# Another order of pools and tiles in SBUF for a transformer kernel on one core

## The chip, the cores and the metric

The kernel runs on one core of one Trainium2 chip. The metric is device time in microseconds of one execution; the time before is the median of three runs, 2584.69 us (2582.28 to 2592.01). TensorE is called PE here, its weight load PEld, VectorE DVE, ScalarE ACT, GpSimd POOL, and the queue that issues the DMAs SP.

## The reference

Two transformer stacks are computed for 256 tokens of width 1024, one after the other. The first has two layers with a context of 256 more tokens (differential and neighbourhood attention, then grouped-query attention; a SwiGLU feed-forward after each). The second has four layers; each is a mixer, a cross-attention to a memory, and a convolved feed-forward, with a layer norm after each:

```python
def swiglu(h, w1, w3, w2):
    return (jax.nn.silu(h @ w1) * (h @ w3)) @ w2

qkv = x @ w_qkv                                   # grouped-query mixer of the second stack
q, k, v = jnp.split(qkv, [A_HEADS * A_HEAD_DIM, (A_HEADS + A_KV_HEADS) * A_HEAD_DIM], axis=-1)
```

Everything is float32. Nearly all of the work is `activation @ weight` with a weight matrix that is read once from DRAM.

## The kernel before, in words

Each large product is made of three matrix products of a cheaper number format (float32r): weight and activation are split into a high and a low part, and `mm3` (L130 to 134) adds high times high (L132), one cross product (L133) and the other (L134). `weights` (L117 to 128) loads 1 MB of a weight matrix into a `raw` buffer by one DMA from SP, and splits it in four quarters: ACT writes `whi` (L126), DVE writes `wlo` (L127). The activations stand transposed, features on partitions, as a pair of tiles high and low (`Th`, `Tl`, in the first phase `xTh`, `xTl`), made by `pair` (L160).

There are two forms of product. In one the weights are the stationary operand (128 columns of `whi` or `wlo`) and the activations move past them, 256 or 512 columns: all "up" products of the feed-forwards, the queries of the cross-attention, the projections of the recurrent layer. In the trace this is `bank<-Th,whi`: the moving operand comes first, the stationary one second. In the other the activations are stationary and 512 columns of weights move (`bank<-whi,Th`, `bank<-whi,hh`): attention projections, output projections, and the "down" products, whose activations `hh`, `hl` are small tiles of the hidden units. `fp32_groups` (L100) does the first two chunks of a stage in plain float32 from `raw` and `xv`.

The program goes through four phases. A (to about 350 us): first mixer. B (350 to 752): feed-forward of 512 tokens, products with 512 moving columns. C (752 to 932): grouped attention with context, and the memory's keys and values. D (932 to the end): the feed-forward of layer two and the whole second stack, 256 tokens. PE's order is the program's order; SP is one queue in order.

SBUF is given out as two stacks that grow towards each other: pools open on the left, from byte 16512 of each partition, or with `side="right"` downwards from byte 229344. A pool that is opened later takes the bytes that a closed pool gave back, and its tiles then wait for the last use of the tiles that overlap them. Left, in order, stand the constants `cp` (19584 bytes), `sm` (1568), `wk` (10240), then per phase `wraw` (`raw`, three buffers of 8 KB), `whl` (`whi` and `wlo`, two buffers of 8 KB each in A and C, three in B and D), then the phase's other tiles. In A and B the activations `xTh`, `xTl`, `Th`, `Tl` are on the right (190.6 to 222.6 KB); in D they are on the left (two pairs, 134.8 to 166.8 KB), with the weights at 70.8 to 118.8 KB. These places are the pools' sizes added up in their order. One thing follows: every left tile behind `sm` begins 32 bytes past a multiple of 128, every right tile 96 bytes past one.

Of the kernel before, what the change touches and what calls it, by code (L numbers as in the profile page):

```python
# [12 lines left out]
F32R = mybir.dt.float32r  # L13
# [45 lines left out]
class Net:  # L59
# [12 lines left out]
    def fill(self, n=1):  # L72
        """Emits n more steps of the work that waits for gaps."""
        while n and self.work:
            if next(self.work[0], None) is None:
                self.work.popleft()
            else:
                n -= 1
# [5 lines left out]
    def flush(self):  # L84
        """Emits the transposes held back until the matrix products that run before them are emitted."""
        while self.held:
            self.held.popleft()()

    def update(self):
        """Emits what is left of the last normalisation: the rows for the next one."""  # L90
        while self.updates:
            self.updates.popleft()()

    def bank(self, tag):
        """A bank of PSUM; several tags: each in turn."""
        i = self.turn[tag] = self.turn.get(tag, -1) + 1
        tag = tag[i % len(tag)]
        return self.psum.tile([P, 512], F32, tag=tag, name="bank" + tag, bufs=1 if tag in "to" else 2)

    def fp32_groups(self, banks, raws, xv, n):  # L100
        """banks[i][:, n-th group of 256, tokens] = raw[:, :, n-th 128 columns]^T @ x, first rows first."""
        for t in range(2):
            ts = slice(t * P, (t + 1) * P)
            for i, (ps, r) in enumerate(zip(banks, raws)):
                for f in range(n):
                    if t or n * i + f == FLUSH:
                        self.flush()
                    for k in range(KD):
                        self.nc.tensor.matmul(ps[:, f * S + t * P : f * S + (t + 1) * P],
                                              r[:, k * n * P + f * P : k * n * P + (f + 1) * P], xv[:, k, ts],  # L110
                                              start=k == 0, stop=k == KD - 1)
# [48 lines left out]
    def pair(self, tag, width):  # L160
        hi = self.tp.tile([P, KD, width], F32R, tag=tag + "h", name=tag + "h")
        lo = self.tp.tile([P, KD, width], F32R, tag=tag + "l", name=tag + "l")
        return hi, lo
# [15 lines left out]
    def fm_rows(self, src, t, n, dst, xv=None, scale=None, bias=None, banks="to", later=None):  # L179
        """Rows src [128, 512] (features 512 n on), transposed, into dst (hi, lo) [:, 4 n.., col]; with xv  # L180
        times scale plus bias by feature, and into xv, too."""
        nc = self.nc
        ps = self.bank(banks[n])
        for i in range(4):
            self.transpose(ps[:, i * P : (i + 1) * P], src[:, i * P : (i + 1) * P])
        hi, lo = (d[:, 4 * n : 4 * n + 4, t * P : (t + 1) * P] for d in dst)
        if xv is None:
            self.split(ps.rearrange("p (k q) -> p k q", k=4), hi, lo)
            return
        for i in range(4):  # L190
            k = 4 * n + i
            p, o = ps[:, i * P : (i + 1) * P], xv[:, i, :]
            if n:
                nc.vector.tensor_scalar(o, p, scale[:, k : k + 1], bias[:, k : k + 1], op0=ALU.mult, op1=ALU.add)
            else:
                nc.scalar.activation(o, p, AF.Identity, scale=scale[:, k : k + 1], bias=bias[:, k : k + 1])
        if later is None:
            self.split(xv, hi, lo)
        else:
            later.append((xv, hi, lo))  # L200

    def modulated(self, src, dst, t, a, b, xv=None, banks="to"):
        """dst (hi, lo) [:, :, t-th tile] = transpose(rms(src)) * a + b; src: a row tile."""
# [11 lines left out]
    def normed_rows(self, src, xv):  # L215
        """xv [128, 8, tokens] = transpose(rms(src)), not yet scaled; src: row tiles."""
# [9 lines left out]
    def scaled(self, xv, dst, cols, a, b):  # L226
        """dst (hi, lo) [:, :, cols] = xv * a + b by feature; xv is overwritten."""
        nc = self.nc
        for k in range(KD):
            x = xv[:, k, cols]  # L230
            (nc.vector if k % 2 else nc.gpsimd).tensor_scalar(x, x, a[:, k : k + 1], b[:, k : k + 1], op0=ALU.mult, op1=ALU.add)
            nc.scalar.activation(dst[0][:, k, cols], x, AF.Copy)
            nc.vector.tensor_tensor(dst[1][:, k, cols], x, dst[0][:, k, cols].bitcast(F32), op=ALU.subtract)

    def conv(self, dst, ps, o, step, n):
        """Two halves of a bank, each with its causal filter of n + 1 taps and bias at o, o + step of fm."""
# [9 lines left out]
    def rope(self, dst, src, width, kind, t):  # L246
        """dst = src * cos + rotated(src) * sin, rows by heads of 64; kind: 0 axial, 1 halves."""
# [88 lines left out]
    def memory(self, pool):  # L336
        """Yields after each chunk of weights."""
# [29 lines left out]
    def ada(self, l, p):  # L367
        """Yields after each chunk of weights; mods[l, p]: by feature, gate rows in DRAM."""
# [42 lines left out]
    def pair_attn(self, q, k, nk, v, out, bias=None, sink=None):  # L411
        """q, k, v: functions of the head's half (v of the key tile, too), q and k as one or as [hi, lo]; out:
        [128, 128] of a bank."""
# [42 lines left out]
    def mixer_ab(self, xT, first, ap, inner, oA, later, after):  # L456
        """ap: pool in inner, which is closed when xT and the first heads are done; later: makes what follows."""
# [140 lines left out]
    def out_ab(self, half):  # L598
        """Weights of half of the rows."""
# [3 lines left out]
    def gated_out(self, oT, ws, res, gate):  # L603
        """res += gate * (o @ w), a row tile; yields after each half of the columns."""
# [11 lines left out]
    def swiglu4(self, xT, res, gates, after):  # L616
        """Hidden units of the first layer's FFN for 512 tokens; res[tt] += gate * out."""
# [48 lines left out]
    def gqa(self, xT, w_qkv, kind, sink, cT=None):  # L666
        """Projections, attention; yields the heads' outputs (hi, lo) by feature tiles."""
# [5 lines left out]
        oT = self.pair("T", S)  # L673
# [107 lines left out]
    def quad_attn(self, qT, kT, v, J, t, g, ops, sink):  # L781
        """Heads (j, i) = 2 x 2 of windowed attention: query tile t, keys of tile t and the one before."""
# [39 lines left out]
    def project(self, parts, w_o, nch, done):  # L822
        """parts yields ((hi, lo), chunks ready); done(t, the two banks of o @ w_o) for each row tile."""
# [38 lines left out]
    def layer_norm(self, i, X, new, last=False, rows=False):  # L862
        """done() for project and ffn: X = norm(ALPHA X + banks), transposed into new() = ((hi, lo), xv);
        rows: (hi, lo) come first, else xv."""
# [124 lines left out]
    def cross(self, xT, xv, w_q):  # L989
        nc = self.nc  # L990
        oT = self.pair("T", S)
# [71 lines left out]
    def rglru(self, xT, xv):  # L1063
        nc, A, fm = self.nc, self.A, self.fm
        uf = self.at.tile([P, KD, S], F32, tag="uf", name="uf", bufs=1)
        uT = self.pair("T", S)
# [52 lines left out]
        oT = self.pair("T", S)  # L1119
# [19 lines left out]
    def mla(self, xT):  # L1139
# [69 lines left out]
        oT = self.pair("T", S)  # L1209
# [69 lines left out]
def tile_kernel(ctx: ExitStack, tc: tile.TileContext, A: dict, out: bass.AP):  # L1279
# [5 lines left out]
    net.cp = sub(ctx, "cp")  # L1285
    net.sm = sub(ctx, "sm", 4)
    net.dr = ctx.enter_context(tc.tile_pool(name="dr", bufs=1, space=DRAM))
    net.wk = sub(ctx, "wk", 2)
# [9 lines left out]
    def scope(name, raw, hl):  # L1298
        st = ExitStack()
        net.wraw = sub(st, name + "r", raw)  # L1300
        net.whl = sub(st, name + "s", hl)
# [3 lines left out]
    with ExitStack() as right:  # L1305
        net.pa = sub(right, "pa", side="right")
        with scope("wA", 3, 2) as st:
            inner, late = ExitStack(), ExitStack()
            xT = [sub(inner, "xT" + n, side="right").tile([P, KD, 2 * S], F32R, name="xT" + n) for n in "hl"]
# [33 lines left out]
            def later():  # L1343
                net.drain()
                net.tp = sub(right, "tA", side="right")
# [12 lines left out]
            def after(tt, oB):  # L1358
# [3 lines left out]
                if tt == NAORD[1]:  # L1362
                    net.drain()
                    ws.append(net.out_ab(1))
                    new.extend(net.pair("T", 2 * S))
# [13 lines left out]
        with scope("wB", 3, 3) as st:  # L1379
# [7 lines left out]
            def after(tt):  # L1387
                if tt == 0:
                    net.drain()
                    new.extend(net.pair("T", 2 * S))  # L1390
# [24 lines left out]
    net.tp = sub(ctx, "tC", 2)  # L1415
    xvp = sub(ctx, "xv")
    newv = lambda: xvp.tile([P, KD, S], F32, tag="xv", name="xv")
    xT, xv = net.pair("T", S), newv()
# [5 lines left out]
    def new():  # L1424
        cur[:] = net.pair("T", S), newv()
# [41 lines left out]
def _cols(w, kt, n):  # L1467
    """[K, N] -> [N / n, K / (128 kt), 128, kt * n]"""
# [5 lines left out]
def _rows(w, kt=2):  # L1474
    """[K, N] -> [K / (128 kt), 128, kt * N]"""
# [4 lines left out]
def _fm(v):  # L1480
    """[n] -> [128, n / 128]"""
# [37 lines left out]
def _qkv(w):  # L1519
    """Query columns in the order of _HEADS, keys and values first."""  # L1520
# [8 lines left out]
def _updown(a, b):  # L1529
    """Two [1024, 2816] side by side in tiles of 128 columns: [22, 128, 2048]"""  # L1530
# [4 lines left out]
def _na_bias(rpb):  # L1535
    """[8, 15, 31] -> [4, 2, 128, 2, 256]: by query and key of the 4 x 64 grid"""
# [91 lines left out]
```

## Time and profile before

| | |
|---|---|
| median of three runs | 2584.69 us |
| profiled execution, span | 2586.1 us |
| PE busy | 2487.0 us, 96% |
| DVE, ACT, POOL busy | 1716.6, 1213.8, 224.4 us |
| DMA | 410 MB read, 161 GB/s over the span |

The span of the profiled execution is 0.05% above the median of the runs, so sums made against it hold for the median. A matmul's duration in the profile is longer than the step from its start to the next one's start, since matmuls are pipelined: 256 columns show 0.28 us and follow each other at 0.12 us. Steps are therefore read from the start times of a timeline.

### The profile page before, as it was taken

To read this page: it belongs to the slowest core of one execution; us is meant where nothing else is said; L and a number is where in the kernel's file an instruction comes from. 1 tells how busy PE (TensorE), PEld (TensorE's weight loads), DVE (VectorE), ACT (ScalarE), POOL (GpSimd) and SP (SyncE) were. 2 spreads that over 40 slices of the span, in tenths; PEclk is the share of its full clock that TensorE was granted. 3 is DMA by queue.
4 is the path that set the end of the run, shared out by engine and by line. 5 is a ranking of instruction groups with operands and counts; after the bars stand their busy time and mean duration, and the time that the engine had idled before them with its cause. 6 is when DMAs were issued, how large, how long until landed. Compare 5 with 4: busy or idle time off the path is not lost.

```text
span 2586.1 us, 39903 instructions
## 1 busy us (share of the span) xinstructions
PE 2487.0 (96%) x15706; PEld 2113.6 (82%) x15706; DVE 1716.6 (66%) x3535; ACT 1213.8 (47%) x2628; POOL 224.4 (9%) x222
## 2 busy tenths in 40 slices
PE   6999999999999999999999988999999999999998
PEld 4867677777778789976899987899878899668998
DVE  5463763334368755478677788677876777886777
ACT  3242442222245554456355565465554455554554
POOL 1000011111100000001100121100102100111000
PEclk8999999999999999999999989999999999999999
DMA  7415234443324355553355445345445455433553
GB/s 319 163 56 213 86 135 171 153 165 142 139 95 150 132 215 183 187 180 119 134 196 183 162 177 196 137 177 193 141 146 186 147 195 180 163 115 133 201 189 114
DMA packets 65612, 418.26 MB, mean 162 GB/s; under 512 B 7424, under 2 KB 9728, under 8 KB 18960
## 3 DMA queue, kind: packets, MB, share of 16 engines
q1 hardware_dynamic: 65424, 415.71, 44.6%
q8 instruction: 123, 2.02, 0.3%
q14 instruction: 65, 0.53, 0.1%
HBM read 410.41 MB, written 5.28 MB: 161 GB/s over the span
## 4 chain that ended last, share of the span: by engine, by line
PE 84%; DVE 9%; ACT 2%; issue 2%; POOL 1%; DMA 1%; POOLq 0%; SPq 0%; DVEq 0%; ACTq 0%
PE banka L132 9%; PE banka L133 9%; PE banka L134 9%; PE banks L134 6%; PE banks L132 6%; PE banks L133 6%; PE bankb L134 5%; PE bankb L132 5%; PE bankb L133 4%; DVE wlo L127 4%; PE bankt L158 3%; PE banko L132 2%; PE banko L134 2%; PE banko L133 2%; PE bankt L133 2%; PE bankt L132 2%
## 5 line engine op out<-in xcount | busy, mean ns | idle before, releaser
L127 DVE TENSOR_TENSOR wlo<-raw,whi 128x512 fp32r<-128x512 f32 (+1 forms) x1184 | 831.7, 729 | 315.5 <-ACT whi L126 312.0
L126 ACT ACTIVATE whi<-raw 128x512 fp32r<-128x512 f32 (+1 forms) x1184 | 662.3, 620 | 669.6 <-issue 179.2
L134 PE MATMUL banks<-Th,wlo 128*128 128x256 f32 x880 | 250.5, 285 | 2.6 <-DVE wlo L127 2.6
L132 PE MATMUL banks<-Th,whi 128*128 128x256 f32 x880 | 250.2, 284 | 0.0
L133 PE MATMUL banks<-Tl,whi 128*128 128x256 f32 x880 | 250.1, 284 | 0.0
L134 PEld LDWEIGHTS banks<-Th,wlo 128*128 128x128 f32 x880 | 169.8, 193 | 3.4 <-DVE wlo L127 3.4
L132 PEld LDWEIGHTS banks<-Th,whi 128*128 128x128 f32 x880 | 170.0, 193 | 0.9
L133 PEld LDWEIGHTS banks<-Tl,whi 128*128 128x128 f32 x880 | 170.0, 193 | 0.8
L133 PE MATMUL banka<-wlo,Th 128*128 128x512 f32 (+1 forms) x304 | 121.6, 403 | 3.6 <-DVE wlo L127 3.6
L132 PE MATMUL banka<-whi,Th 128*128 128x512 f32 (+1 forms) x304 | 123.1, 408 | 1.8 <-ACT Th L150 1.6
L134 PE MATMUL banka<-whi,Tl 128*128 128x512 f32 (+1 forms) x304 | 119.8, 401 | 4.7 <-DVE Tl L151 4.7
L646 DVE TENSOR_TENSOR sg<-sg,bankb 128x512 f32<-128x512 f32 x22 | 15.1, 688 | 164.6 <-PE bankb L134 164.6
L132 PE MATMUL bankt<-Th,whi 128*128 128x256 f32 x424 | 120.3, 284 | 0.0
L132 PE MATMUL banko<-Th,whi 128*128 128x256 f32 x424 | 120.0, 283 | 0.0
L134 PE MATMUL bankt<-Th,wlo 128*128 128x256 f32 x424 | 120.0, 283 | 0.0
L134 PE MATMUL banko<-Th,wlo 128*128 128x256 f32 x424 | 120.0, 283 | 0.0
L133 PE MATMUL banko<-Tl,whi 128*128 128x256 f32 x424 | 120.0, 283 | 0.0
L133 PE MATMUL bankt<-Tl,whi 128*128 128x256 f32 x424 | 120.0, 283 | 0.0
L168 POOL TENSOR_SCALAR rs<-mv 128x1 f32<-128x1 f32 x24 | 7.5, 312 | 1240.3 <-DVE mv L882 1240.2
L132 PE MATMUL bankb<-Th,whi 128*128 128x256 f32 (+1 forms) x344 | 114.9, 335 | 0.0
L134 PE MATMUL bankb<-Th,wlo 128*128 128x256 f32 (+1 forms) x344 | 114.7, 334 | 0.0
L133 PE MATMUL bankb<-Tl,whi 128*128 128x256 f32 (+1 forms) x344 | 114.3, 332 | 0.0
(483 smaller groups left out, 6476.3 us busy)
## 6 DMA issues: line engine op xcount, KB each, us to landing
raw<-in_f_w_up_dram SPq DMA_DIRECT2D x88, 1024.0 KB, 4.8
raw<-in_ffn_w_dram SPq DMA_DIRECT2D x66, 1024.0 KB, 4.9
adaw<-in_ada_w_dram SPq DMA_DIRECT2D x48, 1024.0 KB, 4.9
raw<-in_f_w_down_dram SPq DMA_DIRECT2D x44, 1024.0 KB, 4.9
raw<-in_x_w_q_dram SPq DMA_DIRECT2D x16, 1024.0 KB, 5.0
raw<-in_x_w_o_dram SPq DMA_DIRECT2D x16, 1024.0 KB, 5.0
raw<-in_w_in_ab_dram SPq DMA_DIRECT2D x12, 1024.0 KB, 6.2
raw<-in_a_w_qkv_dram SPq DMA_DIRECT2D x12, 1024.0 KB, 4.9
```

The costliest lines, as they stand in the source:

```text
L126: nc.scalar.activation(hi[:, a:b], r[:, a:b], AF.Copy)
L127: nc.vector.tensor_tensor(lo[:, a:b], r[:, a:b], hi[:, a:b].bitcast(F32), op=ALU.subtract)
L132: mm(out, l[0], r[0], start=start, stop=False)
L133: mm(out, l[0], r[1], start=False, stop=False)
L134: mm(out, l[1], r[0], start=False, stop=stop)
L158: self.nc.tensor.transpose(out, src, self.ident[:k, :k])
L168: nc.gpsimd.tensor_scalar(rs, ssum, scale, eps, op0=ALU.mult, op1=ALU.add)
L646: nc.vector.tensor_tensor(sg, sg, ps[1], op=ALU.mult)
```

## The change

One tile `T` of 32 KB, on the right and opened first, takes all activation pairs; `pair` hands out its halves in turn (or the whole, for 512 tokens). Within it, high and low parts of a pair stand one behind the other. In phase C alone the attention's output still has a pool of its own (`tB`, one tile of 16 KB). The pools `cp`, `sm` and `wk` move to the right, below `T`. In each phase's `scope` the split weights `whl` are opened before `wraw`, so they begin at the left end.

```diff
-    def pair(self, tag, width):
-        hi = self.tp.tile([P, KD, width], F32R, tag=tag + "h", name=tag + "h")
-        lo = self.tp.tile([P, KD, width], F32R, tag=tag + "l", name=tag + "l")
-        return hi, lo
+    def pair(self, width):
+        if self.tp is not None:
+            x = self.tp.tile([P, 2 * KD * width], F32R, tag="T", name="T")
+        else:
+            i = self.turn["T"] = self.turn.get("T", -1) + 1
+            n = 2 * KD * width
+            o = i * n % (4 * KD * S)
+            x = self.acts[:, o : o + n]
+        x = x.rearrange("p (a k w) -> p a k w", a=2, k=KD)
+        return x[:, 0], x[:, 1]
...
-    net.cp = sub(ctx, "cp")
-    net.sm = sub(ctx, "sm", 4)
+    net.acts = sub(ctx, "act", side="right").tile([P, 4 * KD * S], F32R, name="T")
+    net.tp = None
+    net.cp = sub(ctx, "cp", side="right")
+    net.sm = sub(ctx, "sm", 4, side="right")
...
-    net.wk = sub(ctx, "wk", 2)
+    net.wk = sub(ctx, "wk", 2, side="right")
...
         st = ExitStack()
+        net.whl = sub(st, name + "s", hl)
         net.wraw = sub(st, name + "r", raw)
-        net.whl = sub(st, name + "s", hl)
         return st
...
-            xT = [sub(inner, "xT" + n, side="right").tile([P, KD, 2 * S], F32R, name="xT" + n) for n in "hl"]
+            xT = net.pair(2 * S)
...
-                net.tp = sub(right, "tA", side="right")
...
-    net.tp = sub(ctx, "tC", 2)
+    net.tp = None
```

The calls `pair("T", n)` become `pair(n)`; the rest of the diff takes comments out. No instruction, transfer or order of the program is added or removed.

Added up in the new order, the places are: `T` 196576 to 229344 (96 bytes past a multiple of 128), `wk` below at 165184, and in B and D `whi` and `wlo` at 16512 to 65664 (0 past a multiple of 128), `raw` at 65664 to 90240. In A and C, with two buffers, `whi` and `wlo` end at 49280 and `raw` at 73856.

## Rows read from the trace of the kernel before

**Rows 1.** The page: busy time of the engines, and the last chain by engine

```profile
PE 2487.0 (96%) x15706; PEld 2113.6 (82%) x15706; DVE 1716.6 (66%) x3535; ACT 1213.8 (47%) x2628; POOL 224.4 (9%) x222
...
PE 84%; DVE 9%; ACT 2%; issue 2%; POOL 1%; DMA 1%; POOLq 0%; SPq 0%; DVEq 0%; ACTq 0%
```

**Rows 2.** Windows: a feed-forward of D; busy PE, PEld, DVE, ACT, POOL, clock, DMA

```profile
2400.00:2560.00 160.00, 160.00 (x1165) 152.33 (x1165) 119.00 (x235) 96.43 (x195) 0.00 (x0) 1.00 0.51 185
```

**Rows 3.** Groups by form on PE, L132, over the span: count, busy us, mean ns

```profile
L132 PE MATMUL banks<-Th,whi 128*128 128x256 f32 x880 | 250.2, 284 | 0.0
L132 PE MATMUL bankt<-Th,whi 128*128 128x256 f32 x424 | 120.3, 284 | 0.0
L132 PE MATMUL banko<-Th,whi 128*128 128x256 f32 x424 | 120.0, 283 | 0.0
...
L132 PE MATMUL banka<-whi,Th 128*128 128x512 f32 x288 | 117.4, 410 | 1.4 <-ACT Th L150 1.3
L132 PE MATMUL banka<-whi,hh 128*128 128x512 f32 x240 | 94.0, 392 | 0.0
...
L132 PE MATMUL bankb<-whi,Th 128*128 128x512 f32 x144 | 57.0, 396 | 0.0
L132 PE MATMUL banka<-whi,xTh 128*128 128x256 f32 x192 | 55.4, 288 | 2.4 <-ACT xTh L232 2.4
...
L132 PE MATMUL bankb<-Th,whi 128*128 128x256 f32 x184 | 52.3, 285 | 0.0
...
L132 PE MATMUL banka<-Th,whi 128*128 128x256 f32 x104 | 29.8, 286 | 0.0
...
L132 PE MATMUL banka<-xTh,whi 128*128 128x256 f32 x64 | 17.7, 276 | 0.0
```

**Rows 4.** Timeline of PE in D, both operands left: start us, duration; 190 steps

```profile
1086.85 0.28 PE L134 MATMUL bankt<-Th,wlo 128*128 128x256 f32 x1
...
1109.65 0.40 PE L132 MATMUL banka<-whi,hh 128*128 128x512 f32 x1
```

**Rows 5.** Timeline of PE in A, operands on opposite sides; 44 steps

```profile
46.10 0.28 PE L132 MATMUL banka<-xTh,whi 128*128 128x256 f32 x1
...
51.09 0.28 PE L134 MATMUL banka<-xTh,wlo 128*128 128x256 f32 x1
```

**Rows 6.** Timeline of PE at the start of B, opposite sides; 13 steps

```profile
355.98 0.28 PE L132 MATMUL bankb<-Th,whi 128*128 128x256 f32 x1
...
357.51 0.28 PE L133 MATMUL bankb<-Tl,whi 128*128 128x256 f32 x1
```

**Rows 7.** Timeline of PE, 512 columns: same side (10 steps), opposite sides (5 steps)

```profile
742.22 0.39 PE L134 MATMUL banka<-whi,hl 128*128 128x512 f32 x1
...
744.49 0.39 PE L132 MATMUL bankb<-whi,hh 128*128 128x512 f32 x1
...
757.42 0.39 PE L132 MATMUL banka<-whi,Th 128*128 128x512 f32 x1
...
758.58 0.39 PE L134 MATMUL banka<-whi,Tl 128*128 128x512 f32 x1
```

**Rows 8.** Timeline of PE in D, both left, moving at 203 KB; 9 steps

```profile
1248.78 0.28 PE L134 MATMUL banko<-xpth,mvl 128*128 128x256 f32 x1
...
1249.86 0.28 PE L134 MATMUL banko<-xpth,mvl 128*128 128x256 f32 x1
```

**Rows 9.** From B to C: timelines of SP and PE, landing of these DMAs

```profile
716.54 2.30 SPq L115 DMA_DIRECT2D raw<-in_w_in_c_dram  x3
...
751.17 0.39 PE L134 MATMUL banks<-whi,hl 128*128 128x512 f32 x1
751.40 0.63 PE L132 MATMUL banka<-whi,Th 128*128 128x512 f32 x2
752.56 0.50 PE L133 MATMUL banka<-wlo,Th 128*128 128x512 f32 x1 [0.54 <-DVE wlo L127]
...
DMA to landing us min/median/max: 4.8/6.5/8.3
```

**Rows 10.** Windows around an idle stretch of PE in D, columns as in rows 2

```profile
1487.00:1497.00 10.00, 5.42 (x24) 4.94 (x24) 9.28 (x16) 5.08 (x11) 4.17 (x4) 0.66 0.29 109
```

More of the change, by code (lines that the diff above doesn't have):

```diff
@@ L672, in gqa @@
         kT, v = (T if cT is None else TT)("kT", [P, 2, nkt * P]), T("gv", [P, nkt, S])
-        oT = self.pair("T", S)
+        oT = self.pair(S)
         kv = [self.bank("a") for _ in range(2)]
@@ L990, in cross @@
         nc = self.nc
-        oT = self.pair("T", S)
+        oT = self.pair(S)
         mk = [self.at.tile([P, KD, S], F32R, name="mk" + n, bufs=1) for n in "hl"]
@@ L1065, in rglru @@
         uf = self.at.tile([P, KD, S], F32, tag="uf", name="uf", bufs=1)
-        uT = self.pair("T", S)
+        uT = self.pair(S)
         def proj(c, tag="s"):
@@ L1118, in rglru @@
         nc.scalar.activation(sq, sq, AF.Sqrt)
-        oT = self.pair("T", S)
+        oT = self.pair(S)
         gelu = []
@@ L1208, in mla @@
             self.copy(qr[:, :, t * P : (t + 1) * P], pt.rearrange("p (g q) -> p g q", g=4))
-        oT = self.pair("T", S)
+        oT = self.pair(S)
         wk = [x.rearrange("p (k n) -> p k n", k=2) for x in self.weights(A["c_w_k"])]
@@ L1364, in after @@
                     ws.append(net.out_ab(1))
-                    new.extend(net.pair("T", 2 * S))
+                    new.extend(net.pair(2 * S))
                 for tt, oB in done:
@@ L1389, in after @@
                     net.drain()
-                    new.extend(net.pair("T", 2 * S))
+                    new.extend(net.pair(2 * S))
                 s = tt // 2
@@ L1414, in tile_kernel @@
     net.load_memory(sub(ctx, "mkv"))
-    net.tp = sub(ctx, "tC", 2)
+    net.tp = None
     xvp = sub(ctx, "xv")
     newv = lambda: xvp.tile([P, KD, S], F32, tag="xv", name="xv")
-    xT, xv = net.pair("T", S), newv()
+    xT, xv = net.pair(S), newv()
     gain = net.gain(1, 1, m[1, 2][1][:, 0, 0, :])
@@ L1424, in new @@
     def new():
-        cur[:] = net.pair("T", S), newv()
+        cur[:] = net.pair(S), newv()
         return cur
```

## The prediction

> **What bounds the kernel now.** I read the page's busy times first, then the chain, then a table by stage. PE is busy for 96% of the span and makes 84% of the chain [rows 1]. In a feed-forward of phase D it is busy for all of 160 us at the full clock, with DVE at 119.00 us and ACT at 96.43 us [rows 2]. So the time follows PE's step from matmul to matmul, and a change that removes no instruction can act only through that step, or through waits that it makes or takes away. DVE has 41 us to spare in those 160, so a PE that is a few per cent quicker meets no other engine.
>
> Then I read the step, from timelines. It is not one number for one form:
>
> - Both operands left, 256 moving columns: 1086.85 to 1109.65 us in 190 steps, 120.0 ns each [rows 4].
> - Opposite sides, 256 columns: 46.10 to 51.09 us in 44 steps, 113.4 ns [rows 5]; 355.98 to 357.51 in 13 steps, 117.7 ns [rows 6].
> - 512 columns: 2.27 us in 10 steps, 227 ns, on the same side; 1.16 us in 5 steps, 232 ns, on opposite sides [rows 7].
>
> The form, the instructions and the clock are the same within each pair of rows; what differs is where the operands lie. So place does count, and the question is what about the place.
>
> Is it the region? In one place of D the moving tile lies at 203 KB, where `xTh` lay in rows 5, with the stationary one far below, at 119 to 135 KB; 9 steps take 1.08 us, 120 ns [rows 8]. That speaks against "the top is fast" and for the other difference that the program's places show: both tiles of rows 4 and of rows 8 begin 32 bytes past a multiple of 128, while in rows 5 and 6 one operand is at 32 and the other at 96. I call the difference modulo 128 the offset: 0 on the same side, 64 across. After the change it is neither: activations at 96, weights at 0, so 32.
>
> **The change part by part.**
>
> *256-column products with moving activations.* L132 has 880 + 424 + 424 + 184 + 104 = 2016 of them with `Th` [rows 3]; 32 + 32 of these are in B and 16 in C, which leaves 1936 in D, and over the three lines of `mm3` 5808. These now take 120.0 ns. No row has an offset of 32, so I bound it by the nearest: 113.4 ns (offset 64) and 120.0 (offset 0); the bounds go further in the rivals. I take 114.5, the mean of 113.4 and 117.7 weighted by how many matmuls lie across the sides: in A 64 + 192 per line, mostly as in rows 5, against 80 in B and C as in rows 6 [rows 3]. Gain: 5808 x 5.5 ns = 32 us; bounds 0 and 38 us.
>
> *512-column products with stationary activations.* 288 + 144 per line [rows 3], less 48 in C, over three lines 1152 in D. If they go the way of rows 7, from 227 to 232 ns, they lose 1152 x 5 ns = 6 us; bounds: a gain of 6 (if the offset helps here as it does at 256 columns) and a loss of 8. The "down" products keep both operands on the left, offset 0: no change, though both now begin at 0 instead of 32; a gain of up to 6.7 ns on some 1850 (12 us) can't be excluded and is not counted. Phases A and B keep activations on the right and weights on the left: nothing taken, 5 us either way.
>
> *The move of `wraw` behind `whl`.* In before, `raw` has the same bytes in every phase, so the first loads of a phase wait for old `raw` buffers alone, which are free early: the loads for C are issued at 716.54, 35 us ahead of C's first matmul at 751.40 [rows 9]. After the change C's `raw` begins at 49280, where B has its second and third `wlo`; these hold the last "down" weights until B's last matmuls at 751.17. So the loads wait for PE, land 4.8 to 8.3 us later [rows 9], are split, and only then C begins. SP is in order, so what C queues behind them (the memory's load, the gate row) waits too, but is not needed first. Price: 5 to 7 us of idle PE. Idle stretches of some 4 us are followed by a lower clock here (0.66 in the window around one [rows 10]), so 1 to 4 us more. I take 8, bounds 0 and 12. A to B and C to D have no such price: there the overlapped tiles (`oA`, C's keys) are last read well before the loads.
>
> *One tile for all pairs.* Reads and writes of a half wait for that half's last users, as they did with two buffers; the order of allocation is the same. I take 0, bounds 3 us either way. The transposes' identity moves from 0 to 96 past a multiple of 128: some 900 of 109 ns, 2 us either way. Other engines' operands begin elsewhere, too; DVE and ACT have room [rows 2], so 0.
>
> Sum: -32 + 6 + 8 = -18 us. On the median: 2584.7 - 18 = 2566 us. The profiled span is 2586.1, 0.05% more; nothing hangs on that.
>
> The Trainium skill, "SBUF — State Buffer", Who interferes with whom, says that PE has two read ports of its own, one for the moving operand and one for the weight load, and that "PE and ACT never wait on anyone"; only the port pair that DVE and GpSimd share is a place of contention. By that rule the place of an operand could not change a matmul's step, and the change would be worth only the price at C's start. Rows 4 to 6 disagree: 113.4, 117.7 and 120.0 ns for one form.
>
> **The rivals.**
>
> *Nothing about place matters*, and the step differs between the phases for some other reason (what stands around the matmuls, not where operands lie). Then 5808 steps stay at 120.0, and only the 8 us remain: 2593 us. For it: rows 5 and 6 have the same places and still differ by 4 ns. Against it: within D the step is 120.0 in every long run, whatever DVE and ACT do beside it. The same time comes out if offset 32 acts like offset 0.
>
> *The step locks to the offset and lands low.* In cycles of 2.4 GHz the steps are 256 + 32 at offset 0 and 256 + 16 at offset 64; for 512 columns about 512 + 32 and 512 + 46. So going from offset 0 to 64 bytes, which are 16 columns, shifts the step by about half of a grid of 32 cycles. At offset 32 the shift would be a quarter: 256 + 8 is 110 ns. 5808 x 10 ns = 58 us, so 2584.7 - 58 + 6 + 8 = 2541 us.
>
> *The step locks to the offset and lands high: slower.* The same grid, but a step of 256 + 8 leaves too little for what costs 16 cycles even in rows 5; the next place is 256 + 40 cycles, 123.3 ns. Then 5808 x 3.3 ns = 19 us more, with 6 and 8: 2618 us. It decides as soon as D's long runs go above about 121 ns, because 14 us are lost elsewhere anyway.
>
> **How the numbers follow.** Chances: my forecast (113 to 118 ns) 0.45, its own range 2556 to 2583; no effect 0.23; lands low 0.15; lands high 0.17. Differences within 0.5% (13 us) can't be told from no change. Faster by more than that: the forecast below about 116 ns (0.33) and the low lock, 0.48. Within: the forecast's rest and no effect, 0.35. Slower: 0.17. The range is 2539 to 2602: it takes in the low lock and no effect with its bounds, and leaves out the high lock.
>
> **What would show it.** Timelines of D: the step of `Th,whi` in long runs (113 to 118 right, 120 no effect, 110 or 123 a lock); `whi,Th` at 227 or 232; `whi,hh` unchanged at 227. SP's issue of C's first loads at about 750 us instead of 716, and an idle PE of 5 us or more behind B's last matmul. The prediction is wrong if the step is the same in A and D after the change at another value than these, or if DVE or ACT instructions change their durations so much that PE waits for them.

## The result, and the profile after

The changed kernel takes 2611.78 us (median of four runs, 2606.81 to 2621.4) against 2588.35 us for the kernel before in the same comparison: a ratio of 1.0093, 95% interval 1.0076 to 1.0111. It is slower by 23 us. The forecast was 2566 us with a range of 2539 to 2602; the sign was wrong and the time lies outside the range.

The page of the changed kernel (busy time of the engines; then the last chain by engine) looks like that of before [rows 1]:

```profile
PE 2505.0 (96%) x15706; PEld 2122.0 (81%) x15706; DVE 1709.2 (66%) x3535; ACT 1214.3 (47%) x2628; POOL 230.0 (9%) x222
...
PE 85%; DVE 8%; POOL 2%; issue 2%; ACT 2%; DMA 1%; POOLq 0%; DVEq 0%; SPq 0%; ACTq 0%
```

A feed-forward of D, in a window as in [rows 2], has 1162 matmuls in 160 us where before had 1165; the stage on which the forecast stood has not changed:

```profile
2420.00:2580.00 160.00, 160.00 (x1162) 152.17 (x1162) 118.15 (x233) 96.44 (x195) 0.00 (x0) 1.00 0.52 185
```

Both programs have the same 15706 matmuls, so I cut both traces at the same numbers of matmuls and compared the time from the first to the last start of each piece (us, worked out from the start times; the last two columns belong to experiments told below):

| matmuls | what | before | after | raw_first | left_32 |
|---|---|---|---|---|---|
| 0 to 1750 | most of A | 295.0 | 296.8 | 299.3 | 294.4 |
| 1750 to 2050 | end of A, start of B | 55.5 | 63.9 | 55.5 | 65.4 |
| 2050 to 3900 | B | 389.1 | 393.5 | 394.6 | 388.8 |
| 3900 to 4050 | end of B, start of C | 26.0 | 36.0 | 26.1 | 36.3 |
| 4050 to 5200 | C | 165.8 | 165.9 | 165.9 | 165.7 |
| 5200 to the end | D | 1637.2 | 1633.2 | 1638.5 | 1618.6 |

So 18.4 of the 20.7 us lie at the two phase boundaries (8.4 and 10.0), 6.2 in A and B, and D gives 4.0 back. Now the lines.

**D.** The timeline of PE, up products as in [rows 4]. The columns are start, duration, engine, line, names, shapes:

```profile
1113.51 0.28 PE L132 MATMUL bankt<-T,whi 128*128 128x256 f32 x1
1113.62 0.29 PE L133 MATMUL bankt<-T,whi 128*128 128x256 f32 x1
...
1114.23 0.28 PE L132 MATMUL bankt<-T,whi 128*128 128x256 f32 x1
...
1114.95 0.28 PE L132 MATMUL bankt<-T,whi 128*128 128x256 f32 x1
```

The steps were all 120 ns before; now they run 116, 125, 116, 124, 118, 121 and repeat after six. Their sum is 0.72 us (1113.51 to 1114.23 to 1114.95), 120.0 ns in the mean. The place does change the single step, and the mean of a period is where it was.

**B.** 512 moving columns of activations: 21 steps in 4.90 us, 233.3 ns, in the kernel after; 23 steps in 5.27 us, 229.1 ns, in the kernel before, whose lines are the second fence:

```profile
559.89 0.39 PE L132 MATMUL banka<-T,whi 128*128 128x512 f32 x1
...
564.79 0.39 PE L132 MATMUL bankb<-T,whi 128*128 128x512 f32 x1
```

```profile
546.69 0.39 PE L133 MATMUL banka<-Tl,whi 128*128 128x512 f32 x1
...
551.96 0.39 PE L132 MATMUL bankb<-Th,whi 128*128 128x512 f32 x1
```

**From B to C.** The timelines of SP and then of PE, to be read beside [rows 9]:

```profile
766.20 12.72 SPq L115 DMA_DIRECT2D raw<-in_w_in_c_dram  x4
```

```profile
766.01 0.39 PE L134 MATMUL banks<-whi,hl 128*128 128x512 f32 x1
769.67 0.66 PE L158 MATMUL bankt<-cst,xn 128*128 128x128 f32 x4 [3.27 <-DVE xn L184]
...
773.16 1.22 PE L132 MATMUL banka<-whi,T 128*128 128x512 f32 x2 [2.40 <-ACT whi L126]
...
776.21 0.80 PE L133 MATMUL banka<-wlo,T 128*128 128x512 f32 x1 [1.62 <-DVE wlo L127]
```

C's first loads are issued 0.2 us behind the start of B's last matmul, as the forecast had it; PE then waits 3.27, 2.40 and 1.62 us. Behind these waits the granted clock is lower, 0.51 in this window (columns as in [rows 2]):

```profile
776.00:782.00 6.00, 5.79 (x14) 4.55 (x15) 5.28 (x10) 2.31 (x5) 1.37 (x2) 0.51 0.38 127
```

That is the level of 1.2 GHz, and twelve steps of 512 columns take 427 ns each instead of some 233: 2.3 us. PE's steps over 0.6 us, which hold its waits, add up to 6.8 us more here than before (8.4 against 1.6). Together that is 9.1 of the 10.0 us.

**From A to B.** B's first loads on SP, after and then before:

```profile
334.12 0.91 SPq L115 DMA_DIRECT2D raw<-in_ffn_w_dram  x2
```

```profile
289.03 0.33 SPq L115 DMA_DIRECT2D raw<-in_ffn_w_dram  x1
```

They come 45 us later, behind loads of the attention's bias that they were ahead of before. This the forecast did not have. But it is not these loads that PE waits for: they land 7.2 us after their issue, near 342, and ACT splits the first of them at 360.60 us, when it is released by PE (`banka` L134), as it was before. What grew are PE's waits for the attention's softmax tile `e`; the first two lines are after (300 to 372 us), the others before (300 to 362 us):

```profile
PE bankt L158 <- DVE e L446: 4.0, 2, 2.0
PE banks L432 <- ACT e L439: 2.8, 2, 2.5
...
PE bankt L158 <- DVE e L439: 1.0, 1, 1.0
...
PE banks L425 <- ACT e L432: 0.5, 1, 0.5
```

PE's own order has changed, too: matmuls 1765 to 2243 and, at C, 3912 to 4056 stand in another order than before; all others are in the same.

### The profile page after: what moved, and what is told of

Read it like the earlier page. It is cut to its first block, busy times and chain, and to the rows that moved or that the text cites. A ratio compares the mean times of both kernels' runs of the same rounds, so it can differ in the third digit from the quotient of the medians.

```text
span 2606.9 us, 39904 instructions
## 1 busy us (share of the span) xinstructions
PE 2505.0 (96%) x15706; PEld 2122.0 (81%) x15706; DVE 1709.2 (66%) x3535; ACT 1214.3 (47%) x2628; POOL 230.0 (9%) x222
## 4 chain that ended last, share of the span: by engine, by line
PE 85%; DVE 8%; POOL 2%; issue 2%; ACT 2%; DMA 1%; POOLq 0%; DVEq 0%; SPq 0%; ACTq 0%
PE banka L132 9%; PE banka L133 9%; PE banka L134 9%; PE banks L132 6%; PE banks L134 6%; PE banks L133 6%; PE bankb L134 5%; PE bankb L133 5%; PE bankb L132 5%; DVE wlo L127 3%; PE bankt L158 3%; PE banko L132 2%; PE banko L134 2%; PE banko L133 2%; PE bankt L132 2%
## 5 line engine op out<-in xcount | busy, mean ns | idle before, releaser
L134 PE MATMUL banks<-T,wlo 128*128 128x256 f32 x880 | 248.2, 282 | 3.0 <-DVE wlo L127 2.9
L132 PE MATMUL banks<-T,whi 128*128 128x256 f32 x880 | 249.5, 284 | 0.0
L133 PE MATMUL banks<-T,whi 128*128 128x256 f32 x880 | 249.2, 283 | 0.0
L132 PE MATMUL banka<-whi,T 128*128 128x512 f32 (+2 forms) x496 | 180.6, 365 | 5.3 <-ACT whi L126 2.4
L133 PE MATMUL banka<-wlo,T 128*128 128x512 f32 (+2 forms) x496 | 177.4, 359 | 6.5 <-DVE wlo L127 6.5
L134 PE MATMUL banka<-whi,T 128*128 128x512 f32 (+2 forms) x496 | 175.7, 358 | 4.1 <-DVE T L151 2.8
L134 PEld LDWEIGHTS banks<-T,wlo 128*128 128x128 f32 x880 | 167.7, 191 | 3.7 <-DVE wlo L127 3.7
L133 PEld LDWEIGHTS banks<-T,whi 128*128 128x128 f32 x880 | 165.9, 188 | 0.8
L132 PEld LDWEIGHTS banks<-T,whi 128*128 128x128 f32 x880 | 165.6, 188 | 0.9
L132 PE MATMUL banka<-T,whi 128*128 128x512 f32 (+1 forms) x392 | 139.0, 354 | 0.0
L134 PE MATMUL banka<-T,wlo 128*128 128x512 f32 (+1 forms) x392 | 137.2, 350 | 0.0
L133 PE MATMUL banka<-T,whi 128*128 128x512 f32 (+1 forms) x392 | 136.5, 348 | 0.0
L653 DVE TENSOR_TENSOR sg<-sg,bankb 128x512 f32<-128x512 f32 x22 | 15.1, 688 | 169.1 <-PE bankb L134 169.1
L132 PE MATMUL bankt<-T,whi 128*128 128x256 f32 x424 | 120.1, 283 | 0.0
L132 PE MATMUL banko<-T,whi 128*128 128x256 f32 x424 | 119.9, 283 | 0.0
L133 PE MATMUL bankt<-T,whi 128*128 128x256 f32 x424 | 119.7, 282 | 0.0
L133 PE MATMUL banko<-T,whi 128*128 128x256 f32 x424 | 119.7, 282 | 0.0
L134 PE MATMUL bankt<-T,wlo 128*128 128x256 f32 x424 | 119.4, 282 | 0.0
L134 PE MATMUL banko<-T,wlo 128*128 128x256 f32 x424 | 119.0, 281 | 0.0
L132 PEld LDWEIGHTS banka<-whi,T 128*128 128x128 f32 x496 | 95.3, 192 | 28.8 <-ACT whi L126 6.5
```

What stands on the lines that cost most here:

```text
L132: mm(out, l[0], r[0], start=start, stop=False)
L133: mm(out, l[0], r[1], start=False, stop=False)
L134: mm(out, l[1], r[0], start=False, stop=stop)
L653: nc.vector.tensor_tensor(sg, sg, ps[1], op=ALU.mult)
```

## The experiments

Below, the distance is the place of the activations minus that of the weights in the 256 bytes that the places repeat by, as these runs came to show. For activations and weights it is 0 in D of the kernel before, 64 in its A and B, and 96 in the changed kernel, but for the attention's output in C (`tB`).

### offset_sweep: products alone, at sixteen pairs of places

```python
for kind in "dabw":
    for om in (0, 32, 64, 96):
        for os in (0, 32, 64, 96):
            case(kind, om, os)      # T[om / 4:], W[os / 4:]
```

> Only the matrix products, with nothing beside them, and no result of the reference's: 64 streams, each of one form of product with the activations at 0, 32, 64 or 96 bytes past a multiple of 128 and the weights at 0, 32, 64 or 96, on opposite sides of SBUF as after the change. Forms: d, the up products of phase D (256 columns, slices of the activations 1024 bytes apart); a, those of A (256 columns, slices 2048 bytes apart); b, those of B (512 columns, 2048 apart); w, moving weights of 512 columns. Theory P (the two offsets modulo 128 decide the step): 120 ns in forms d and a where they are equal, 113 to 118 ns at activations 96 and weights 32, a mean of 118 to 120 at 96 and 0; 227 ns for form w at equal offsets, 231 to 235 at others. Rival Q (the distance of the slices decides): form d is at 120 ns for every offset, form a at 113. Rival U (what stands around the products in the kernel, waits and other engines): one step for all offsets and both forms of 256 columns.

With no other engine at work, forms d and a have the same step at every pair, so the distance of the slices plays no part (rival Q). The step is not one number (rival U): 120.0 ns wherever both are equal, 120.1 at activations 96 and weights 0, 117.8 at 96 and 32, and 116.7 to 118.4 at the rest. Pairs of equal difference agree: 0 and 32, 32 and 64, 64 and 96 all give 118.4. The pair of the changed kernel is one of the worst. Windows of 10 us of form d (columns as in [rows 2], PE's count second) at activations 0 and weights 0, and at 64 and 32:

```profile
38.00:48.00 10.00, 10.00 (x86) 10.00 (x85) 0.00 (x0) 0.00 (x0) 0.00 (x0) 1.00 0.01 2
140.00:150.00 10.00, 10.00 (x88) 10.00 (x87) 0.00 (x0) 0.00 (x0) 0.00 (x0) 1.00 0.01 2
```

### raw_first: the order of the two pools undone

```diff
+        net.wraw = sub(st, name + "r", raw)
         net.whl = sub(st, name + "s", hl)
-        net.wraw = sub(st, name + "r", raw)
```

> The changed kernel with raw opened before the split weights again, nothing else. Theory O (the order of these two pools costs both phase boundaries): the first loads of B at about 289 us and those of C at about 716 again, 7 us back between A and B and 10 between B and C, 2595 us, 17 less than the changed kernel. Rival O2 (only the loads of C are held up by it, what A to B lost comes from the pairs in one tile): 2602. Rival O3 (the loads come late for another reason): 2612, no change.

2597.11 us (ten runs), ratio to before 1.0017 (1.0004 to 1.0031); the changed kernel had 1.0093. Both boundaries are as before (55.5 and 26.1 us in the table), all 15706 matmuls are in the order of before, and the loads on SP come early again:

```profile
293.67 0.33 SPq L115 DMA_DIRECT2D raw<-in_ffn_w_dram  x1
...
726.52 2.30 SPq L115 DMA_DIRECT2D raw<-in_w_in_c_dram  x3
```

Theory O holds: two lines that swap two pools cost 18 us at two places. Of these, 9 are left between the two profiled executions, because A, B and D of raw_first are 2.5, 1.1 and 5.3 us longer than after the change; between the two ratios lie 0.8%. Whether the order of SP or that of PE costs the 8.4 us from A to B was not tested apart, since both came back together.

### left_32: the weights moved by 32 bytes

```diff
+    sub(ctx, "pad").tile([P, 8], F32, name="pad")
     net.acts = sub(ctx, "act", side="right").tile([P, 4 * KD * S], F32R, name="T")
```

> The changed kernel with one tile of 32 bytes at the left end, so the weights begin 32 bytes past a multiple of 128 and the activations stay at 96, as they stood in A and B of the kernel before. Theory P (the two offsets modulo 128 decide): 113 to 118 ns instead of 120 for 5808 products of D, 12 to 39 us less, and A's 113 ns back, 3 us: 2570 to 2597 us. Rival Q (the distance of the slices or another trait of D decides): D stays at 120.0, A and B gain 3 to 7 us: 2605 to 2609.

2593.06 us (ten runs), ratio 1.0008 (0.9995 to 1.0020): 19 us less than the changed kernel, for 32 bytes that hold nothing. The same products of D now follow each other at 117.9 ns (47 steps in 5.54 us):

```profile
1104.39 0.28 PE L132 MATMUL bankt<-T,whi 128*128 128x256 f32 x1
...
1109.93 0.28 PE L134 MATMUL bankt<-T,wlo 128*128 128x256 f32 x1
```

A and B are back at 294.4 and 388.8 us, and the boundaries keep their price (65.4 and 36.3), so the two causes are separate.

### before_t64: the kernel before, its activations of D moved by 64 bytes

```diff
+    sub(ctx, "pad0").tile([P, 16], F32, name="pad0")
     net.tp = sub(ctx, "tC", 2)
+    sub(ctx, "pad1").tile([P, 16], F32, name="pad1")
```

> The kernel before with one tile of 64 bytes ahead of the pool of the activations of D and one of 64 bytes behind it, so that in D the activations alone move, from 32 to 96 bytes past a multiple of 128; they stay on the left. Theory P: D's step falls from 120 to 113 to 118 ns, 12 to 39 us less, 2546 to 2573 us, with 512 moving weight columns at 231 to 234 instead of 229. Rival Q, or one by sides (left beside left is slow): 120.0 ns as before, 2585 to 2590 us.

2578.43 us, ratio 0.9949 (0.9934 to 0.9964). D's up products run at 117.6 ns in the mean, and all operands are still on the left: the slow step does not come from the side. The end of some down products (17 steps in 3.96 us) and the up products behind them (18 in 2.12):

```profile
1083.81 0.39 PE L133 MATMUL banka<-wlo,hh 128*128 128x512 f32 x1
...
1087.77 0.28 PE L132 MATMUL bankt<-Th,whi 128*128 128x256 f32 x1
...
1089.89 0.28 PE L132 MATMUL bankt<-Th,whi 128*128 128x256 f32 x1
```

Two things came unasked. The down products, whose operands keep the same place in 128 bytes, rose from 227.8 to 233.3 ns; their activations had moved by 128 bytes. So 128 is not the period. And the steps alone (up 13 us less, down 7 more, `whi,T` 4.5 more) make 2 us, where D became 15 shorter. The rest is idle time: steps of PE longer than 0.6 us add up to 69.3 us in D before and to 56.5 here. At a layer norm, before in the first two lines, before_t64 in the others:

```profile
1286.00:1296.00 10.00, 8.39 (x75) 8.16 (x75) 8.98 (x16) 4.22 (x10) 4.50 (x5) 1.00 0.31 107
1296.00:1306.00 10.00, 7.24 (x53) 7.05 (x52) 6.18 (x12) 2.27 (x4) 0.17 (x1) 0.83 0.73 231
```

```profile
1284.50:1294.50 10.00, 10.00 (x79) 9.46 (x79) 8.20 (x13) 4.70 (x10) 9.09 (x8) 1.00 0.30 106
1294.50:1304.50 10.00, 7.95 (x69) 7.69 (x68) 6.43 (x12) 2.77 (x6) 0.42 (x1) 1.00 0.82 266
```

Before, PE is idle for 1.6 and for 2.8 us, and then has a granted clock of 0.83; here it is idle once, for some 2 us, and the clock stays at 1.00.

### distance_sweep: one operand moved through 512 bytes

```python
for kind in "dbw":
    for om in range(0, 512, 32):
        case(kind, (base + om) % 512, 0)
```

> Only the matrix products again, no result of the reference's. The weights stay, the activations begin 0, 32, ... 480 bytes further on, for the forms d (up products of D, 256 columns), b (512 columns) and w (512 moving weight columns); then 4 to 28 bytes in steps of 4 for d and w. The first sweep left 120, 117.8 and 116.7 ns to be explained by the distance of the operands alone, and the kernel before_t64 had down products at 233 ns whose operands lie 128 bytes apart modulo 256. Theory P256 (the distance modulo 256 decides): 120 and 226.7 ns at 0 and 256, 233 ns at 128 for forms b and w, and the values of 0 to 224 come again at 256 to 480. Rival P128 (modulo 128): 120 and 226.7 ns at 128 and 384 too. Rival P512: 256 differs from 0.

Windows of 10 us, columns as in [rows 2], form d, at distances 0, 64, 96, 128, 192, 256 and 448. The figure to read is the second, PE's count (a matmul that is partly in the window counts):

```profile
26.00:36.00 10.00, 10.00 (x85) 10.00 (x85) 0.00 (x0) 0.00 (x0) 0.00 (x0) 1.00 0.00 0
...
60.50:70.50 10.00, 10.00 (x87) 10.00 (x86) 0.00 (x0) 0.00 (x0) 0.00 (x0) 1.00 0.01 2
72.00:82.00 10.00, 10.00 (x85) 10.00 (x85) 0.00 (x0) 0.00 (x0) 0.00 (x0) 1.00 0.00 0
83.00:93.00 10.00, 10.00 (x87) 10.00 (x86) 0.00 (x0) 0.00 (x0) 0.00 (x0) 1.00 0.01 2
...
106.00:116.00 10.00, 10.00 (x91) 10.00 (x90) 0.00 (x0) 0.00 (x0) 0.00 (x0) 1.00 0.01 2
...
128.00:138.00 10.00, 10.00 (x86) 10.00 (x85) 0.00 (x0) 0.00 (x0) 0.00 (x0) 1.00 0.01 2
...
196.50:206.50 10.00, 10.00 (x90) 10.00 (x90) 0.00 (x0) 0.00 (x0) 0.00 (x0) 1.00 0.01 2
```

And 512 moving weight columns at distances 0 (17 steps in 3.85 us, 226.5 ns), 64 (33 in 7.70, 233.3) and 192 (38 in 8.70, 228.9):

```profile
402.07 0.39 PE L1350 MATMUL w<-W,T 128*128 128x512 f32 x1
...
405.92 0.39 PE L1351 MATMUL w<-W,T 128*128 128x512 f32 x1
...
418.51 0.40 PE L1352 MATMUL w<-W,T 128*128 128x512 f32 x1
...
426.21 0.39 PE L1352 MATMUL w<-W,T 128*128 128x512 f32 x1
...
463.28 0.39 PE L1352 MATMUL w<-W,T 128*128 128x512 f32 x1
...
471.98 0.39 PE L1351 MATMUL w<-W,T 128*128 128x512 f32 x1
```

The second half of each stream, mean step in ns; 256 to 480 repeat the row of 0 to 224 within 0.3 ns:

| distance | 0 | 32 | 64 | 96 | 128 | 160 | 192 | 224 |
|---|---|---|---|---|---|---|---|---|
| 256 columns of activations move | 120.0 | 117.8 | 117.8 | 120.1 | 118.7 | 117.4 | 113.3 | 118.3 |
| 512 columns of activations move | 226.7 | 233.3 | 228.8 | 233.4 | 233.5 | 234.1 | 233.4 | 233.4 |
| 512 columns of weights move | 226.7 | 233.4 | 233.4 | 234.6 | 232.3 | 233.4 | 228.7 | 233.3 |

P256 holds. The last two rows are nearly each other's mirror image (64 in one is 192 in the other, 160 is 96), so what counts is the moving operand's place minus the stationary one's. Of two places the first sweep gave a second value: 117.8 at 192, where it is 113.3 here, and 116.7 at one of three pairs with 32. A third is in the kernel: at a distance of 64 its A ran at 113.4 ns [rows 5], where both sweeps, and D in left_32 and before_t64, have 117.8. So the distance alone does not fix the step everywhere.

### raw_first_left_32, best_places and before_t192: the table put to use

The first has the edits of raw_first and left_32. The second adds, in D alone,

```diff
+    sub(ctx, "pad1").tile([P, 32], F32, name="pad1")
     ctx.enter_context(scope("wD", 3, 3))
```

The third is the kernel before with

```diff
+    sub(ctx, "pad0").tile([P, 48], F32, name="pad0")
     net.tp = sub(ctx, "tC", 2)
```

> The changed kernel with raw opened first and the tile of 32 bytes at the left end. Theory (the two costs are independent: pool order at the phase boundaries, distance of the operands in the stages): the 15 us of raw_first and the 19 us of left_32 add up, 2578 us. Rival (a PE that is faster in A and B meets the waits for loads and splits that the other edit leaves, so part is lost): 2584 to 2592 us.

> As raw_first_left_32, and in D 128 bytes more ahead of the weights, so that there the activations lie 64 bytes below the weights modulo 256 instead of 64 above. In the first sweep both distances gave 117.8 ns for the up products, but 228.9 ns at one and 233.3 at the other for 512 moving weight columns. Theory P256: some 1056 of these products fall from 233.5 to 229 ns, 5 us less than raw_first_left_32: 2573 us. Rival (only the distance modulo 128 counts): no difference to it, 2578.

> The kernel before with one tile of 192 bytes ahead of the pool of the activations of D and none behind it, so that in D the activations and all that lies behind them (the hidden units) are 192 bytes further on than the weights. Theory P256: up products at 117.8 ns (13 us less than before), 512 moving weight columns at 229 for both other forms (3 us more), so 2581 us from the steps; the idle stretches of PE at the layer norms, which were 10 us shorter in before_t64, are not in that sum and could make it 2570. Rival P128 gives the same, except that the products with hidden units would behave as in before_t64 if their 128 bytes were no distance at all (233 ns).

They gave 2572.31 us (ratio 0.9942, 0.9919 to 0.9964), 2569.14 (0.9923, 0.9907 to 0.9940) and 2555.39 (0.9877, 0.9847 to 0.9907), against 2587.09 for before. The two edits add up (1.5% off the changed kernel, 0.8 and 0.8 alone). In best_places `whi,T` fell from 233.5 to 230.0 ns as expected; its pad also moved D's `raw`, D's loads came later, and C took 170.9 us instead of 165.8, which took that gain back. And before_t192, whose up products in D were expected at 117.8 ns, runs them at 113.5 (20 steps in 2.27 us), 114.0 in the mean, which is 22 us less over 5808 products:

```profile
1004.20 0.28 PE L132 MATMUL banks<-Th,whi 128*128 128x256 f32 x1
...
1006.47 0.28 PE L134 MATMUL banks<-Th,wlo 128*128 128x256 f32 x1
```

It is the fastest kernel of this study: 192 bytes of nothing, 1.2%. What the steps make of D can be summed for each kernel from the mean step of its 5808 up products, 1056 `w,T` and 1320 down products behind 965 us (stalls left out), with the change of its idle stretches over 0.6 us beside it (us, all against before):

| kernel | up, ns | w,T, ns | down, ns | from steps | idle | sum | D measured |
|---|---|---|---|---|---|---|---|
| before | 119.9 | 229.2 | 227.8 | | | | |
| after | 120.0 | 233.9 | 228.2 | +6.1 | -9.0 | -2.9 | -4.0 |
| raw_first | 120.0 | 234.0 | 228.2 | +6.2 | -4.1 | +2.1 | +1.3 |
| left_32 | 117.8 | 233.5 | 228.1 | -7.3 | -7.7 | -15.0 | -18.6 |
| before_t64 | 117.6 | 233.5 | 233.3 | -1.6 | -12.8 | -14.4 | -15.1 |
| before_t192 | 114.0 | 230.2 | 229.1 | -31.5 | -2.7 | -34.2 | -36.5 |

Steps and idle stretches together tell D of these kernels to 4 us. The idle stretches vary by up to 13 us from kernel to kernel, but each is that of one execution, and executions of one kernel lie up to 18 us apart (before_t192); no run was made to find what sets them.

### history, t192_h0, t192_h192 and t192_h64: which of two steps

At a distance of 192 best_places has 116.9 ns and before_t192 114.0. I took what runs ahead of a stream to choose.

```python
for q in (192, 64, 160):
    for p in (0, 64, 128, 192):
        case("w", base + p, 0)
        case("d", base + q, 0)
```

> Only the matrix products, no result of the reference's. The up products of D at a distance of 192, 64 and 160 bytes (activations past weights, modulo 256), each time right behind 48 products with 512 moving weight columns at a distance of 0, 64, 128 or 192. At a distance of 192 the first sweep showed 117.8 ns and the second 113.3, and D ran at 114 ns in before_t192 and at 117 in best_places. Theory H (a stream keeps the step it falls into, and what ran before it decides which): at 192, 113.3 ns behind some of the predecessors, behind the one at 192 at least, and 117.8 behind others, behind the one at 0 at least; 64 and 160 the same or with two values of their own. Rival (what stands beside the products in a kernel decides, not the predecessor): one value behind all four.

Windows in the streams of form d at 192, behind products with moving weights at 0, 64, 128 and 192:

```profile
47.00:57.00 10.00, 10.00 (x88) 10.00 (x87) 0.00 (x0) 0.00 (x0) 0.00 (x0) 1.00 0.00 0
69.00:79.00 10.00, 10.00 (x91) 10.00 (x90) 0.00 (x0) 0.00 (x0) 0.00 (x0) 1.00 0.01 2
91.00:101.00 10.00, 10.00 (x87) 10.00 (x87) 0.00 (x0) 0.00 (x0) 0.00 (x0) 1.00 0.01 2
113.00:123.00 10.00, 10.00 (x87) 10.00 (x86) 0.00 (x0) 0.00 (x0) 0.00 (x0) 1.00 0.01 2
```

So there are two steady steps, 113.3 ns behind 64 and 117.8 behind the others, with nothing else running: history counts. That the one at 192 leads to 113.3 was wrong. Streams at 64 had 117.8 behind all four, and those at 160 had 118.6 to 118.7, where distance_sweep had 117.4. The next two kernels have activations at 192 in every phase (raw first, `cp` and `sm` left of the weights) and differ in the place of D's hidden units:

```diff
+    sub(ctx, "pad2").tile([P, 48], F32, name="pad2")    # t192_h192; [P, 16] in t192_h64
     xvp = sub(ctx, "xv")
```

> The changed kernel with raw opened first and the constants and statistics on the left again, which puts the activations 192 bytes past the weights modulo 256 in every phase; hidden units stay at a distance of 0. Against best_places (2569 us): C to D without the 5 us that its pad ahead of D cost, 4 us more in B (233.3 instead of 229 ns for 960 products). Theory H: D's up products, which follow down products at distance 0, stay near 117 ns: 2568 us. Rival (the lock in best_places was chance): 114 ns in D, 2551 us.

> As t192_h0, with one tile of 192 bytes in D ahead of the hidden units, so that they lie 192 bytes past the weights too, as in before_t192. Theory H: up products of D at 114 ns instead of 117 (5808 of them, 17 us less), down products at 229 instead of 227 (1320, 3 us more): 14 us less than t192_h0, 2554 us. Rival (the lock is chance, or comes from activations and weights on the same side): 3 us more than t192_h0.

2569.44 us (ratio 0.9943, 0.9924 to 0.9961) and 2567.68 (0.9937, 0.9916 to 0.9959): no difference that can be measured, where 14 us were expected. In the profiled execution of t192_h0 the up products go to 117.8 ns in all five feed-forwards, though other stretches of D come down to 113.3; in that of t192_h192 three feed-forwards stay at 113.6 and two at 117.8. By their mean steps D of t192_h192 should be some 6 us shorter, and it is 0.9 longer. Two of its feed-forwards: 117.6 ns (25 steps in 2.94 us) and 113.5 (26 in 2.95):

```profile
1002.08 0.28 PE L133 MATMUL banko<-T,whi 128*128 128x256 f32 x1
...
1005.02 0.28 PE L134 MATMUL banko<-T,wlo 128*128 128x256 f32 x1
...
1369.73 0.28 PE L132 MATMUL banks<-T,whi 128*128 128x256 f32 x1
...
1372.68 0.28 PE L134 MATMUL banks<-T,wlo 128*128 128x256 f32 x1
```

> As t192_h192, with 64 bytes instead of 192 ahead of the hidden units. Theory H2 (a stream at a distance of 192 has two steady steps, 113.3 and 117.8 ns; products with moving weights at a distance of 192 keep whichever there is, those at 0 lead to 117.8, those at 64 to 113.3, as in the run named history): the up products of all five feed-forwards at 113.3 to 114 ns, where t192_h192 had three of five there (113.6 in three, 117.8 in two, 115.3 in the mean: 9 us less now), and the down products at 233.3 ns instead of 229.5 (1320, 5 us more): 2564 us, 4 less than t192_h192. Rival (chance chooses the step at the start of each feed-forward): again some feed-forwards at 117.8, 2571 us or more.

2569.48 us (ratio 0.9924, 0.9907 to 0.9940), closer to the rival. Up products are at 115.2 ns in the mean, and at 113.4 to 117.8 by stretches of 40 us, in every feed-forward. Products at 64 ahead of a stream do not choose in the kernel as they did alone. What chooses between 113.3 and 117.8 stays open; that there are these two, and that hidden units at 0 led to the slower one in all five feed-forwards of t192_h0, is what the runs show.

## Why the prediction was wrong

**What bounds the kernel** was right: PE, by its step and by its waits. Durations of 0.28 us hide this entirely, and only start times show it.

**The step of the 256-column products** is the term that failed: 114.5 ns forecast, 120.0 measured. The prediction found the right trait, the difference of the two places, in two pairs of rows [rows 4, 5], but took it modulo 128 and without its sign. With 256 bytes as the period, the changed kernel stands at 96, not at "32", and 96 has 120 ns in the mean like 0. The forecast of 114.5 was a mean of 113.4 and 117.7, two steps that were both read at a distance of 64, and there was no row at the changed kernel's own; in the table neighbours 32 bytes apart differ by up to 5 ns in either direction, so a neighbour's step tells little. Even at 64, D has 117.8 (left_32) and 117.6 (before_t64), which would be 13 us. The 32 us of gain were 0. The forecast's bounds (0 and 38 us) did hold this; the rival "no effect" had its number right for D, and its main reason wrong: place matters, and these two places are equally slow, as its last sentence allowed. That "lands high" has 2618 us, the nearest to the 2612 measured, is luck: its step of 123.3 ns did not come, and the boundaries cost 18 us instead.

The rule of the Trainium skill ("SBUF — State Buffer", Who interferes with whom), that PE never waits on anyone, is about engines that overlap in time. The prediction read it as one for PE's own two operands, too, and by that reading there would have been only the price at C. offset_sweep shows more plainly than rows 4 to 6 that the reading does not hold: with all other engines idle the step goes from 116.7 to 120.1 ns by place alone.

**The 512-column products** were near: `whi,T` rose by 4.7 ns (5 forecast), on 1056 products in D and not 1152. For "phases A and B: nothing taken, 5 us either way" the trace has 6.2 us more, 1.8 and 4.4. Their distance went from 64 to 96, which the table prices at 229 to 233 ns; the 1152 products of A and B with 512 moving columns of activations make 5 us of it.

**The move of `wraw`** was right in its mechanism at C, to the place of the issue, and a little low: 10.0 us against 8, inside its bounds. The split was right, too: 6.8 us of waits (5 to 7 forecast) and 2.3 us by the lower clock (1 to 4). "A to B has no such price" was wrong by 8.4 us. The working asked only whether the overlapped bytes are free in time, and they are: the second of B's buffers takes the low half of `oA`, last read near 286 us. But the compiled order of SP is not fixed by the program's text: with other places, B's loads came behind all eight loads of the bias instead of one. The same holds for PE, whose order the text before the prediction calls the program's: at both boundaries it changed as well. So the step that failed is that the order stays, and not that the bytes are free. raw_first shows that the order of the two pools is the cause; why the compiled order comes out so was not tested, and that PE's new order is what lengthens its waits for `e` (6.8 us against 1.5) is likely from the rows and not shown.

**One tile for all pairs, at 0,** was not tried alone; raw_first keeps that tile and has both boundaries as before, so nothing is left for it to explain there.

**D's idle stretches** were no term at all, and in the profiled executions they gave 9 us back. Without that the changed kernel would have lost some 30 us.

Put together: 0 instead of -32, 5 for `whi,T`, 6 in A and B, 10 and 8 at the boundaries, and 9 back, makes 20, of 20.7 in the traces.

## What to carry to other kernels

When a layout changes, compare the two operands' places of each hot matmul before and after, moving minus stationary in 256 bytes, and read the step from start times. A tile of 32 to 192 empty bytes is a cheap experiment and was worth up to 1.2% here. And ask of each pool not only whether its bytes are free when the next phase loads, but compare the compiled order of the queue and of PE around each boundary with that of before.

## What the runs showed of the hardware

- PE's step for float32r products depends on the distance of its two operands, with period 256 bytes and nothing else running: 113.3 to 120.1 ns for 256 columns at multiples of 32 bytes, 226.7 to 234.6 for 512. The distance 0, one of the two worst for 256 columns, is the best for 512.
- Within 32 bytes it goes on: in distance_sweep, form d took 123.4 ns at 4 bytes, 116.6 at 16 and 122.2 at 20.
- At one distance there can be two steady steps, in the kernel kept over hundreds of products: 113.3 and 117.8 ns at 192 (history, t192_h192), and 113.4 and 117.8 at 64 (A of the kernel before, D of left_32).
